# A hybrid attention, HGRN2 and mixture-of-experts layer: weights split by halves, experts gathered from x, slots 64 to 95 gathered in a branch, a ring of 20 pieces

## The chip, the cores and the metric

The kernel runs on one core of a Trainium2 chip. The metric is the device time of one execution in microseconds, and less is better. Three executions of the kernel before took 1235.04, 1236.87 and 1237.81 us; their median, 1236.87 us, is the time before.

## What is computed

One layer of an encoder over 256 tokens of 1024 channels, all in float32. The first half normalises x, modulates it by a vector c, multiplies it by `w_in` (1024 x 5632), sends the parts through differential attention and a chunkwise HGRN2 recurrence, multiplies both results by `w_branch_a` and `w_branch_b` (512 x 1024), merges them by sigmoid gates and multiplies by `w_out` (1024 x 1024). The second half is a mixture of 32 experts, of which each token takes the best 4:

```python
def expert_block(args):
    toks, e = args
    xb = xf[toks]
    gu = xb @ w_gate_up[e] + b_gate_up[e]
    g, u = jnp.split(gu, 2, axis=-1)
    g = jnp.minimum(g, SWIGLU_LIMIT)
    u = jnp.clip(u, -SWIGLU_LIMIT, SWIGLU_LIMIT)
    glu = g * jax.nn.sigmoid(g * SWIGLU_ALPHA)
    return ((u + 1.0) * glu) @ w_down[e] + b_down[e]
...
h = rms_norm(x, norm_pre_ffn[l]) * (1.0 + sc2) + sh2
y = moe(h, router_w[l], router_b[l], w_gate_up[l], b_gate_up[l], w_down[l], b_down[l])
x = x + g2 * rms_norm(y, norm_post_ffn[l])
```

`w_gate_up` of one expert is 1024 x 2048 and `w_down` 1024 x 1024, 12 MiB together, so the experts' weights are 384 MiB.

## The kernel before

**The ring.** All large weights arrive in pieces of 128 x 2048 float32, 1 MiB each. `piece(i)` is one of 16 tiles of the arena (`NA`) or one of `NM` = 2 more in the pool `mo`, which takes the memory of the pool `late` once that is closed (L863). The deque `slots` holds the numbers of the pieces in use as a ring: `chunk` (L84) takes the next one through `spot` and issues a DMA from SyncE's queue at L87. SyncE's queue is in order, so an issue that waits for its piece to be free holds up all issues behind it. In the token mixer the ring is short (`use(8, 9, 6, 10, 3)`, L358), because other pieces hold intermediate results; it grows by `slots.insert` as these die: 3, 5, 2, 4, 0, then 1 and 6 after the branch projections, then 14, 15, 11, 12, 13 and 7 (L861) and the two of `mo` when the mixer is over. For the experts it has 18 pieces.

**The mixer.** A float32 weight is split into a rounded part `hi` and a rest `lo`, and each product is three matmuls of the type float32r (`mm3`, L139 to L141). `split` (L116) does a whole piece at a time: a copy on ScalarE (L119) into one of three tiles `hi`, a subtraction on VectorE (L122) into one of the pieces 11, 12 and 13. `split_between` (L125) does the same in two halves at three places. `proj` (L301) then goes through a piece at a time, and for each through both blocks of 128 tokens. The router's end is L776 to L846: transposes, logits, the largest four, and `posm`, the place (1, 2, ...) of each token among those of its expert. At L833 ScalarE writes `xn2`, the second norm of x, 128 x 2 x 1024.

**The experts.** Expert e's tokens are taken out of `xn2` by a matmul with a one-hot matrix. `onehot` (L898) compares `posm` with a row of numbers on VectorE for two experts at a time and for 96 places of each (`CA` = 96, `EB` = 2); `gather` (L910) then multiplies: 128 x 128 blocks of `xn2` are the weights, 192 one-hot columns move. ScalarE and VectorE (L907, L908) scale the result into `xg`. The gathers for the experts e+2 and e+3 are put as `fill` between the two products of the experts e and e+1, two quarters each (experts 0 and 1 do it otherwise: L1099 and the list `first` for experts 0 and 1, all four quarters for experts 2 and 3 in expert 1).

The number of tokens of an expert is read into registers of TensorE, ScalarE and VectorE by `load(e + 1)` (L1105) behind the fills of expert e. Branches then choose the work. Up to 32 tokens take the path of 32 (L958, L983), more the path of 64 (L948, L975), and those from 65 to 96 take a second path of 32 besides (`po`, `so`, `gdo`). A count over 96 goes to `rare`. Per expert there are two halves of `gate_up`, each followed by its branches (L1158, L1164), the fills, the load of the next count, then under branches (L1191, L1195) the transposes of the activations (L967) and of the gates (`turned`, L997), `down` and the combination (`combine`, L1000: matmuls at L1007 and sums into `acc` on VectorE at L1010). `step` and `in_turn` write TensorE's order out by hand: halves, fills, load, down. The PSUM pools are `psa` (4 banks), `psb` and `psc` (2 each): `turned` and the first transposes take theirs from `psc` and `psb`, as the four banks of `combine` do.

```python
pcs = [bank((psc, psb)[c // 2], NT, 256) for c in range(4)]
order = range(4) if n == U else (0, 2, 1, 3)
...
for g in fill:
    in_turn(g)
if e < NE - 1:
    after = in_turn(lambda: load(e + 1))
    wd = down_loads(e)
```

## Time and profile before

| | |
|---|---|
| median of three runs | 1236.87 us |
| the profiled execution | 1234.81 us |
| its span, first to last instruction | 1232.7 us |
| TensorE busy | 1003.6 us (81%) |
| VectorE / ScalarE busy | 422.8 us (34%) / 225.4 us (18%) |
| moved by DMA | 465.70 MB, 378 GB/s over the span |
| granted TensorE clock, mean | 0.933 of full speed |

The profiled execution is 2.06 us under the median. PE is TensorE's matmuls, PEld its weight loads, DVE is VectorE, ACT ScalarE, SPq the queue of SyncE that issues the DMAs. An "idle before" in square brackets is the time in which an engine did nothing ahead of a row, with what ended it. A matmul in float32 stands in the trace as two instructions. [...]

### The profile page before, as it was taken

What the parts mean: (1) busy time and instruction counts of PE and PEld (TensorE: products, weight loads), DVE (VectorE), ACT (ScalarE), POOL (GpSimd) and SP (SyncE); (2) the same over time, 40 slices, a digit from 0 to 9 for tenths busy, and PEclk for the clock granted to TensorE, in tenths of its full rate; (3) what the DMA queues carried; (4) which work ended last, traced back from release to release, by engine and by line L of the source; (5) the groups of instructions that cost most, each with busy time, mean ns of one, the idle gap of its engine ahead of it and who ended that gap; (6) DMA issues with size and microseconds to landing.
All of it is one profiled execution on the core that took longest, in us unless ns stands there. A gap on an engine that the chain in (4) does not pass through costs nothing. (4 is left out here: it accounts for less than half of the span.)

```text
span 1232.7 us, 17243 instructions
## 1 busy us (share of the span) xinstructions
PE 1003.6 (81%) x6774; PEld 520.9 (42%) x6774; DVE 422.8 (34%) x784; ACT 225.4 (18%) x401; POOL 26.0 (2%) x36
## 2 busy tenths in 40 slices
PE   6999989998779998887789879769776667777855
PEld 3777777874334333333333334323232222233312
DVE  3597789642222222323222232312222212122212
ACT  3553565341111000110000010000010000010001
POOL 1020000010000000000000000000000000000000
PEclk9998989989899999998999999988999887889978
DMA  9966668699999999799999999999999999999994
GB/s 352 317 220 226 230 244 319 263 374 379 394 421 422 423 422 422 308 403 377 422 421 423 422 422 422 423 422 425 422 421 421 423 422 422 416 415 421 419 417 173
DMA packets 100191, 465.70 MB, mean 378 GB/s; under 512 B 9716, under 2 KB 9814, under 8 KB 67256
## 3 DMA queue, kind: packets, MB, share of 16 engines
q1 hardware_dynamic: 100024, 463.31, 93.1%
q8 instruction: 125, 2.05, 0.6%
q14 instruction: 42, 0.34, 0.1%
HBM read 462.23 MB, written 1.05 MB: 376 GB/s over the span
## 5 line engine op out<-in xcount | busy, mean ns | idle before, releaser
L958 PE MATMUL bank<-piece,xg 128*32 128x512 f32 x1472 | 206.6, 673 | 65.0 <-DMA piece<-in_w_gate_up_dram 51.2
L948 PE MATMUL bank<-piece,xg 128*64 128x512 f32 x768 | 171.0, 597 | 3.8 <-PEq L1158 3.0
L1010 DVE TENSOR_TENSOR acc<-acc,bank 128x512 f32<-128x512 f32 x136 | 84.3, 681 | 247.0 <-PE bank L1007 247.0
L926 DVE TENSOR_SCALAR bank<-bank 128x256 f32<-128x256 f32 (+1 forms) x35 | 18.3, 524 | 368.2 <-PE bank L958 254.6
L958 PEld LDWEIGHTS bank<-piece,xg 128*32 128x32 f32 x1472 | 44.4, 116 | 204.7 <-DMA piece<-in_w_gate_up_dram 112.0
L948 PEld LDWEIGHTS bank<-piece,xg 128*64 128x64 f32 x768 | 56.1, 138 | 112.0 <-issue 101.0
L983 PE MATMUL bank<-piece,actT 128*32 128x256 f32 x1472 | 99.5, 421 | 4.1 <-DMA piece<-in_w_down_dram 2.0
L927 ACT ACTIVATE s<-bank 128x256 f32<-128x256 f32 (+1 forms) x32 | 14.8, 463 | 476.5 <-DVE bank L926 476.5
L916 PEld LDWEIGHTS bank<-oh,xn 128*128 128x128 f32 x512 | 86.2, 200 | 30.6 <-issue 20.8
L916 PE MATMUL bank<-oh,xn 128*128 128x192 f32 (+1 forms) x512 | 95.4, 342 | 0.4 <-DVE xg L908 0.4
L975 PE MATMUL bank<-piece,actT 128*64 128x512 f32 x384 | 85.0, 595 | 0.9
L139 PE MATMUL bank<-hi,piece 128*128 128x512 f32 x208 | 82.5, 403 | 2.5 <-ACT hi L119 2.5
L140 PE MATMUL bank<-piece 128*128 128x512 f32 x208 | 82.6, 397 | 2.1 <-DVE piece L122 2.1
L141 PE MATMUL bank<-hi,piece 128*128 128x512 f32 x208 | 82.6, 397 | 0.0
L983 PEld LDWEIGHTS bank<-piece,actT 128*32 128x32 f32 x1472 | 49.8, 121 | 48.4 <-issue 16.7
L967 PE MATMUL bank<-ident,s 128*128 128x128 f32 x88 | 16.9, 298 | 62.8 <-issue 30.5
L122 DVE TENSOR_TENSOR piece<-piece,hi 128x2048 fp32r<-128x2048 f32 x27 | 62.7, 2324 | 14.3 <-ACT hi L119 14.3
L1007 PE MATMUL bank<-y,gt 32*128 32x256 f32 (+1 forms) x544 | 49.2, 396 | 21.3 <-ACT y L1026 21.3
L119 ACT CAST hi<-piece 128x2048 fp32r<-128x2048 f32 x27 | 51.2, 1900 | 18.9 <-PE bank L141 16.2
L1007 PEld LDWEIGHTS bank<-y,gt 32*128 32x128 f32 (+1 forms) x544 | 33.4, 185 | 44.5 <-ACT y L1026 42.4
L975 PEld LDWEIGHTS bank<-piece,actT 128*64 128x64 f32 x384 | 26.5, 137 | 51.7 <-issue 46.8
L1026 ACT COPY y<-bank 128x256 f32<-128x256 f32 (+1 forms) x35 | 15.6, 445 | 176.8 <-PE bank L983 95.0
(267 smaller groups left out, 884.9 us busy)
## 6 DMA issues: line engine op xcount, KB each, us to landing
piece<-in_w_gate_up_dram SPq DMA_DIRECT2D x256, 1024.0 KB, 19.7
piece<-in_w_down_dram SPq DMA_DIRECT2D x128, 1024.0 KB, 19.6
piece<-in_w_in_dram SPq DMA_DIRECT2D x22, 1024.0 KB, 6.3
piece<-in_w_mod_dram SPq DMA_DIRECT2D x16, 1024.0 KB, 6.4
piece<-in_w_mod_dram SPq DMA_DIRECT2D x16, 512.0 KB, 6.9
piece<-in_w_out_dram SPq DMA_DIRECT2D x4, 1024.0 KB
piece<-in_w_branch_b_dram SPq DMA_DIRECT2D x2, 1024.0 KB
piece<-in_w_branch_a_dram SPq DMA_DIRECT2D x2, 1024.0 KB
```

The source lines that it names most:

```text
L119: (seq if order else now)(A, lambda: nc.scalar.copy(hi, v))
L122: (seq if order else now)(V, lambda: nc.vector.tensor_tensor(lo, v, hi.bitcast(F32), ALU.subtract))
L139: nc.tensor.matmul(out, ah, bh, start=start, stop=False, skip_group_check=True)
L140: nc.tensor.matmul(out, ah, bl, start=False, stop=False, skip_group_check=True)
L141: return nc.tensor.matmul(out, al, bh, start=False, stop=stop, skip_group_check=True)
L916: last = nc.tensor.matmul(ph[:, j], xn2[:, t, k * P : (k + 1) * P], oh[:, t, cs], start=t == 0, stop=t == NT - 1)
L948: nc.tensor.matmul(pp[r : r + C], xg[:, k, :C], wg[k][:, 0, 512 * q : 512 * (q + 1)], start=False, stop=k == KD - 1, skip_group_check=True)
L958: nc.tensor.matmul(halves(po[U * q : U * q + U]), xg[:, k, s0 : s0 + U], quarter(wg[k][:, 0], q), start=False, stop=k == KD - 1, skip_grou ...
L975: nc.tensor.matmul(py[C * n : C * n + C], at[:, j, C * half : C * half + C], wd[kk // 2][:, kk % 2, 512 * n : 512 * (n + 1)], start=kk == ...
L983: nc.tensor.matmul(py[U * c : U * c + U, 0:256], at[:, j, U * q : U * q + U], wd[kk // 2][:, kk % 2, 256 * c : 256 * (c + 1)], start=kk == ...
L1007: nc.tensor.matmul(pcs[c][:, t], gt[r : r + n, t * P : (t + 1) * P], y[r : r + n, w : w + 256], start=True, stop=True)
L1010: nc.vector.tensor_tensor(acc[:, :, cs], acc[:, :, cs], pcs[c], ALU.add)
```

## The change

The ring has two pieces more; several tiles are smaller, moved or gone, and the order of some work is another.

- `split` always works by halves: `hi` and `lo` are tiles of 128 x 1024 with four buffers each, both in `late`, so that pieces 11, 12 and 13 are no longer taken. 12 and 13 join the mixer's ring at once, and 11 holds what `xn2` held and joins after the branch projections. `proj`, the branch projections and the first half of `w_out` go through their weights by pairs of 128 rows, and for each pair through both blocks of tokens.
- `xn2` after the router is gone: the gather multiplies x, and the one-hot holds each token's factor `r2` in place of 1.
- `onehot` and `gather` cover 64 places of each of two experts (128 columns, not 192). Places 64 to 95 are gathered by `gather_more` into `xo`, under a branch of its own behind the load of the next expert's count (`ahead`).
- `NM` is 4; `w2` is made in expert 30 in a buffer of `xg`.
- `turned` writes to a bank of `psa`, and the combination of the path of 32 goes in the order 2, 0, 3, 1.

```diff
@@ -40,7 +40,7 @@
-NM = 2
+NM = 4
@@ -109,30 +109,20 @@
-    now = lambda engine, f: f()
-
-    parts = deque((11, 12, 13))
-
-    def split(v, n, m, order=False):
-
-        hi = late.tile([P, 2048], F32R, name="hi", bufs=3).rearrange("p (a b) -> p a b", b=m)
-        (seq if order else now)(A, lambda: nc.scalar.copy(hi, v))
-        lo = piece(parts[0], F32R).rearrange("p (a b) -> p a b", b=m)
-        parts.rotate(-1)
-        (seq if order else now)(V, lambda: nc.vector.tensor_tensor(lo, v, hi.bitcast(F32), ALU.subtract))
-        return hi, lo
-
-    def split_between(v, m, before):
-
-        hi = late.tile([P, 2048], F32R, name="hi", bufs=3).rearrange("p (a b) -> p a b", b=m)
-        lo = piece(parts[0], F32R).rearrange("p (a b) -> p a b", b=m)
-        parts.rotate(-1)
+    def split(v, before=None, order=False):
+
+        now = seq if order or before else lambda engine, f: f()
+        parts = [], []
         for i in range(2):
-            before(i)
+            if before:
+                before(i)
+            hi, lo = (late.tile([P, 2, 512], F32R, name=n, bufs=4) for n in ("hi", "lo"))
             h = slice(2 * i, 2 * i + 2)
-            seq(A, lambda: nc.scalar.copy(hi[:, h], v[:, h]))
-            seq(V, lambda: nc.vector.tensor_tensor(lo[:, h], v[:, h], hi[:, h].bitcast(F32), ALU.subtract))
-        return hi, lo
+            now(A, lambda: nc.scalar.copy(hi, v[:, h]))
+            now(V, lambda: nc.vector.tensor_tensor(lo, v[:, h], hi.bitcast(F32), ALU.subtract))
+            for part, t in zip(parts, (hi, lo)):
+                part.extend((t[:, 0], t[:, 1]))
+        return parts
@@ -182,7 +172,8 @@
-    xn2 = const.tile([P, NT, D], F32, name="xn2")
+    xn2 = part(11, 0, NT, D)
+    r2 = const.tile([P, NT], F32, name="r2")
@@ -293,19 +284,19 @@
-        for kh, (wh, wl) in enumerate(w):
+        for K in range(0, KD, 2):
+            wh, wl = w[K // 4]
...
-                for k in range(4):
-                    K = 4 * kh + k
-                    mm3(pp[t], (hTh[:, K, ts], hTl[:, K, ts]), (wh[:, k], wl[:, k]), K == 0, K == KD - 1)
+                for k in (K, K + 1):
+                    mm3(pp[t], (hTh[:, k, ts], hTl[:, k, ts]), (wh[k % 4], wl[k % 4]), k == 0, k == KD - 1)
@@ -369,8 +360,8 @@
-    wf = split_between(wf, 512, lambda i: normed_split(2 + i, f[i]))
-    wq = split_between(win_chunk(3, 1), 512, lambda i: None)
+    wf = split(wf, lambda i: normed_split(2 + i, f[i]))
+    wq = split(win_chunk(3, 1), order=True)
@@ -698,14 +689,17 @@
-        wb, wa = [split(chunk(rows(a[w], 0, 4)[:, :, ns], 4, 512), 4, 512) for w in ("w_branch_b", "w_branch_a")]
+        wb, wa = [split(chunk(rows(a[w], 0, 4)[:, :, ns], 4, 512)) for w in ("w_branch_b", "w_branch_a")]
+        for (wh, wl), (yh, yl), sig in ((wb, yT[0], sigb), (wa, yT[1], siga)):
+            pp = [bank(psa) for t in range(NT)]
+            for h0 in range(0, H, 2):
+                for t in range(NT):
+                    ts = slice(t * P, (t + 1) * P)
+                    for h in (h0, h0 + 1):
+                        last = mm3(pp[t], (yh[:, h, ts], yl[:, h, ts]), (wh[h], wl[h]), h == 0, h == H - 1)
+            for t in range(NT):
+                nc.vector.tensor_tensor(sig[:, t, ns], pp[t], sig[:, t, ns], ALU.mult)
         for t in range(NT):
-            ts = slice(t * P, (t + 1) * P)
-            for (wh, wl), (yh, yl), sig in ((wb, yT[0], sigb), (wa, yT[1], siga)):
-                pp = bank(psa)
-                for h in range(H):
-                    last = mm3(pp, (yh[:, h, ts], yl[:, h, ts]), (wh[:, h], wl[:, h]), h == 0, h == H - 1)
-                nc.vector.tensor_tensor(sig[:, t, ns], pp, sig[:, t, ns], ALU.mult)
@@ -713,6 +707,7 @@
+    slots.insert(4, 11)
@@ -800,8 +795,10 @@
+    for K in range(0, KD, 2):
+        for t in range(NT):
+            times(t, (K, K + 1))
     for t in range(NT):
-        times(t, range(KD))
@@ -827,10 +824,8 @@
-    r21 = rstd(mx[:, 1])
+    r21 = rstd(mx[:, 1], r2[:, 1:2])
     largest(0, pl0, r20)
-    for t, r2 in enumerate((r20, r21)):
-        seq(A, lambda: nc.scalar.activation(xn2[:, t], x[:, t], AF.Copy, scale=r2))
@@ -858,14 +853,14 @@
-    for i, t in enumerate((14, 15, 11, 12, 13, 7)):
+    for i, t in enumerate((14, 15, 7)):
...
-        slots.insert(8 + i, NA + i)
+        slots.insert(5 + i, NA + i)
@@ -892,20 +887,21 @@
-        return nc.vector.tensor_tensor(oh, iota[:, None, s0 : s0 + n].to_broadcast([P, ne, n]),
-                                       posm[:, t, e0 : e0 + ne].unsqueeze(2).to_broadcast([P, ne, n]), ALU.is_equal)
-
-    def onehot(e0, ne, s0, n):
-        oh = mo.tile([P, NT, EB, CA], F32, name="oh")
-        oh = oh.rearrange("p t e c -> p t (e c)")[:, :, : ne * n].rearrange("p t (e c) -> p t e c", c=n)
+
+        for i in range(ne):
+            last = nc.vector.tensor_scalar(oh[:, i], iota[:, s0 : s0 + n], posm[:, t, e0 + i : e0 + i + 1], r2[:, t : t + 1], ALU.is_equal, ALU.mult)
+        return last
+
+    def onehot(oh, e0, ne, s0, n):
+        oh = oh.rearrange("p t c -> p (t c)")[:, : NT * ne * n].rearrange("p (t e c) -> p t e c", t=NT, c=n)
...
-        nc.scalar.activation(xg[:, k, cs], ph[:, 0], AF.Identity, bias=sh2[:, k : k + 1], scale=sa2[:, k : k + 1])
-        nc.vector.tensor_scalar(xg[:, k + 1, cs], ph[:, 1], sa2[:, k + 1 : k + 2], sh2[:, k + 1 : k + 2], ALU.mult, ALU.add)
+        nc.scalar.activation(xg[:, k, cs], ph[0], AF.Identity, bias=sh2[:, k : k + 1], scale=sa2[:, k : k + 1])
+        nc.vector.tensor_scalar(xg[:, k + 1, cs], ph[1], sa2[:, k + 1 : k + 2], sh2[:, k + 1 : k + 2], ALU.mult, ALU.add)
@@ -913,14 +909,24 @@
-                last = nc.tensor.matmul(ph[:, j], xn2[:, t, k * P : (k + 1) * P], oh[:, t, cs], start=t == 0, stop=t == NT - 1)
-        gathered(ph, xg, kp, cs)
+                last = nc.tensor.matmul(ph[:, j], x[:, t, k * P : (k + 1) * P], oh[:, t, cs], start=t == 0, stop=t == NT - 1)
+        gathered([ph[:, 0], ph[:, 1]], xg, kp, cs)
...
-        xg = mo.tile([P, KD, EB * CA], F32, name="xg")
-        oh = onehot(e0, EB, 0, CA)
+        xg = mo.tile([P, KD, EB * C], F32, name="xg")
+        oh = onehot(mo.tile([P, NT, EB * C], F32, name="oh"), e0, EB, 0, C)
         return xg, [lambda kp=kp: gather(oh, xg, kp) for kp in range(KD // 2)]
+
+    def gather_more(e, xo):
+
+        oh = onehot(mo.tile([P, NT, U], F32, name="oho", bufs=1), e, 1, C, U)
+        ph = [bank(psc, KD // 2, U) for i in range(2)]
+        for k in range(KD):
+            for t in range(NT):
+                nc.tensor.matmul(ph[k % 2][:, k // 2], x[:, t, k * P : (k + 1) * P], oh[:, t], start=t == 0, stop=t == NT - 1)
+        for kp in range(KD // 2):
+            gathered([ph[i][:, kp] for i in range(2)], xo, kp, slice(0, U))
@@ -1000,7 +1006,7 @@
-        order = range(4) if n == U else (0, 2, 1, 3)
+        order = (2, 0, 3, 1) if n == U else (0, 2, 1, 3)
@@ -1020,15 +1026,15 @@
-        turned(gd, gt, bank(psc) if pt is None else pt)
+        turned(gd, gt, pt)
@@ -1129,25 +1134,38 @@
-    after = load(0)
-    fin = pt = other = None
+    def ahead(e):
+
+        cnt = in_turn(lambda: load(e))
+        xo = mo.tile([P, KD, U], F32, name="xo", bufs=1)
+        with tc.If(cnt > C) as more:
+            gather_more(e, xo)
+        step(more.cond_inst)
+        return cnt, xo
+
+    after = ahead(0)
+    fin = other = None
...
-        cnt = after
+        cnt, xo = after
...
-        if e == LASTS:
-            w2 = mo.tile([P, D], F32, name="w2", bufs=1)
-            for n, pr in enumerate(rows_of(gw2, psc)):
-                nc.scalar.copy(w2[:, 512 * n : 512 * (n + 1)], pr)
...
+            if e == NE - 2:
+                w2 = mo.tile([P, KD, EB * C], F32, name="xg").rearrange("p a b -> p (a b)")
+
+                def gated_rows():
+                    for n, pr in enumerate(rows_of(gw2, psc)):
+                        nc.scalar.copy(w2[:, 512 * n : 512 * (n + 1)], pr)
+
+                fill = [gated_rows]
...
-        xe = xg[:, :, j * CA : (j + 1) * CA]
+        xe = xg[:, :, j * C : (j + 1) * C]
@@ -1156,7 +1174,7 @@
-                gate_up_32(e, po, xe, wg, ks, C)
+                gate_up_32(e, po, xo, wg, ks)
@@ -1182,10 +1200,11 @@
-            after = in_turn(lambda: load(e + 1))
+            after = ahead(e + 1)
...
-            pt, other = bank(psa), bank(psa)
+            other = bank(psa)
+        pt = bank(psa)
```

## Rows read from the trace of the kernel before

**Rows 1.** The page's slices of the span, 40 of 30.8 us: DMA in tenths, GB/s
```profile
DMA  9966668699999999799999999999999999999994
GB/s 352 317 220 226 230 244 319 263 374 379 394 421 422 423 422 422 308 403 377 422 421 423 422 422 422 423 422 425 422 421 421 423 422 422 416 415 421 419 417 173
```

**Rows 2.** Windows: span, busy time of PE, PEld, DVE, ACT, POOL, clock, DMA share, GB/s
```profile
30.00:262.00 232.00, 219.85 (x1119) 176.27 (x1118) 171.29 (x233) 114.77 (x152) 17.70 (x12) 0.96 0.74 265
...
160.00:170.00 10.00, 9.12 (x34) 8.01 (x35) 7.95 (x16) 4.64 (x10) 0.00 (x0) 0.50 0.67 205
...
375.00:557.00 182.00, 164.26 (x1038) 69.64 (x1030) 46.67 (x92) 17.67 (x39) 0.00 (x0) 1.00 0.97 400
...
510.00:520.00 10.00, 7.34 (x84) 3.69 (x78) 2.90 (x5) 1.12 (x3) 0.00 (x0) 1.00 0.30 126
530.00:540.00 10.00, 9.68 (x47) 3.19 (x44) 0.00 (x0) 0.00 (x0) 0.00 (x0) 1.00 0.96 361
560.00:570.00 10.00, 8.38 (x56) 2.50 (x60) 0.15 (x1) 0.00 (x0) 0.00 (x0) 0.69 0.75 288
600.00:1200.00 600.00, 451.68 (x3441) 191.11 (x3443) 140.49 (x298) 54.45 (x129) 0.00 (x0) 0.92 1.02 421
```

**Rows 3.** Waits of SyncE's queue, 500 to 580 us: in total, times, longest
```profile
SPq L87 <- PE bank L975: 28.5, 8, 14.2
...
SPq L87 <- PE bank L958: 13.6, 7, 8.7
```

**Rows 4.** Timeline of PE, experts 7, 8 and 9: start, us
```profile
504.46 2.87 PE L916 MATMUL bank<-oh,xn 128*128 128x192 f32 x16
...
508.53 0.41 PE L997 MATMUL bank<-ident,gdo 128*128 128x128 f32 x2 [0.99 <-DVE xg L908]
...
516.27 0.63 PE L967 MATMUL bank<-ident,s 128*128 128x128 f32 x4 [2.05 <-DVE acc L1010]
...
546.38 0.63 PE L967 MATMUL bank<-ident,s 128*128 128x128 f32 x4 [1.26 <-DVEq L1191]
...
561.11 0.62 PE L938 MATMUL bank<-bgu,sel 96*32 96x512 bf16 x4 [3.98 <-issue]
561.51 5.98 PE L958 MATMUL bank<-piece,xg 128*32 128x512 f32 x32
```

**Rows 5.** Timeline of PE, experts 0 and 1: gathers of 96 and of 192 columns
```profile
289.83 2.02 PE L916 MATMUL bank<-oh,xn 128*128 128x96 f32 x16
...
314.69 5.71 PE L916 MATMUL bank<-oh,xn 128*128 128x192 f32 x32
```

**Rows 6.** Groups of the experts, 265 to 1233 us: busy us, mean ns, idle before
```profile
L1010 DVE TENSOR_TENSOR acc<-acc,bank 128x512 f32<-128x512 f32 x136 | 84.3, 681 | 247.0 <-PE bank L1007 247.0
...
L927 ACT ACTIVATE so<-bank 128x256 f32<-128x256 f32 x3 | 1.1, 383 | 57.5 <-DVE bank L926 57.5
```

**Rows 7.** Branches on PE, line 1195: duration ns least/median/most
```profile
L1195 PEldq COMPARE_BRANCH  x44: 65/218/5052, 294.5 to 1212.7; - x44
```

**Rows 8.** Groups of the mixer, 0 to 265 us: busy us, mean ns, idle before
```profile
L122 DVE TENSOR_TENSOR piece<-piece,hi 128x2048 fp32r<-128x2048 f32 x27 | 62.7, 2324 | 14.3 <-ACT hi L119 14.3
L119 ACT CAST hi<-piece 128x2048 fp32r<-128x2048 f32 x27 | 51.2, 1900 | 18.9 <-PE bank L141 16.2 <-DMA piece<-in_w_in_dram 2.6
...
L134 DVE TENSOR_TENSOR piece<-piece,hi 128x1024 fp32r<-128x1024 f32 x6 | 7.2, 1220 | 0.4 <-ACT hi L133 0.3
L133 ACT CAST hi<-piece 128x1024 fp32r<-128x1024 f32 x6 | 6.1, 1042 | 0.0
```

**Rows 9.** Timeline of PE in the mixer: two waits for a split, products in a row
```profile
158.62 0.72 PE L139 MATMUL bank<-hi,piece 128*128 128x512 f32 x2 [2.47 <-ACT hi L119]
...
197.18 0.50 PE L140 MATMUL bank<-piece 128*128 128x512 f32 x1 [1.74 <-DVE piece L122]
197.52 0.39 PE L141 MATMUL bank<-hi,piece 128*128 128x512 f32 x1
197.75 0.39 PE L139 MATMUL bank<-hi,piece 128*128 128x512 f32 x1
```

More of the change, by code (lines that the diff above doesn't have):

```diff
@@ L295, in win_half @@
     def win_half(i, kh, order=False):
-        return split(win_chunk(i, kh), 4, 512, order)
+        return split(win_chunk(i, kh), order=order)
     def win(i, order=False):
@@ L316, in proj_T @@
                 K = 4 * kh + k
-                last = mm3(pp[h // 2][:, h % 2], (wh[:, k, hs], wl[:, k, hs]), (hTh[:, K], hTl[:, K]), K == 0 and h % 2 == 0, K == KD - 1)
+                last = mm3(pp[h // 2][:, h % 2], (wh[k][:, hs], wl[k][:, hs]), (hTh[:, K], hTl[:, K]), K == 0 and h % 2 == 0, K == KD - 1)
         return last
@@ L357 @@
     wf = win_chunk(4, 1)
-    use(8, 9, 6, 10, 3)
+    use(12, 13, 8, 9, 6, 10, 3)
     ph = [transposed_cols(xn2, kp, psc) for kp in (2, 3)]
@@ L730, in w_out_half @@
         ns = slice(512 * n, 512 * (n + 1))
-        wo = [split(chunk(rows(a["w_out"], 512 * kh, 4)[:, :, ns], 4, 512), 4, 512) for kh in range(2)]
+        wo = [split(chunk(rows(a["w_out"], 512 * kh, 4)[:, :, ns], 4, 512)) for kh in range(2)]
         def times(t, ks):
@@ L1027, in out_of, with rest_of @@
         combine(gt, y, n) if fin is None else combine_into(fin, gt, y, n)
-    def rest_of(e, s0, xr, spare):
-        ring = deque(spare[1:])
+    def rest_of(e, s0, spare):
+        ring = deque(spare[2:])
         def half(w, kh, n):
@@ L1038, in half @@
             return v
-        oh = onehot(e, 1, s0, P)
+        xr = part(piece(spare[1]), 0, KD, P)
+        oh = onehot(mo.tile([P, NT, EB * C], F32, name="oh"), e, 1, s0, P)
         for kp in range(KD // 2):
@@ L1083, in rare @@
                 with tc.If(cnt > CA):
-                    rest_of(e, CA, xr, spare)
+                    rest_of(e, CA, spare)
                     with tc.If(cnt > CA + P):
-                        rest_of(e, CA + P, xr, spare)
+                        rest_of(e, CA + P, spare)
         return some
-    xg = mo.tile([P, KD, EB * CA], F32, name="xg")
-    oh = mo.tile([P, NT, EB, CA], F32, name="oh")
+    xg = mo.tile([P, KD, EB * C], F32, name="xg")
+    oh = mo.tile([P, NT, EB * C], F32, name="oh")
     for t in range(NT):
-        seq(V, lambda: slot_is(oh[:, t], t, 0, EB, 0, CA))
+        seq(V, lambda: slot_is(oh[:, t].rearrange("p (e c) -> p e c", c=C), t, 0, EB, 0, C))
     count()
-    oh = oh.rearrange("p t e c -> p t (e c)")
-    ph = [bank((psc, psb)[kp % 2], 2, CA) for kp in range(KD // 2)]
+    ph = [bank((psc, psb)[kp % 2], 2, C) for kp in range(KD // 2)]
     for t in range(NT):
         for k in range(KD):
-            seq(T, lambda: nc.tensor.matmul(ph[k // 2][:, k % 2], xn2[:, t, k * P : (k + 1) * P], oh[:, t, 0:CA], start=t == k % 2 == 0,
+            seq(T, lambda: nc.tensor.matmul(ph[k // 2][:, k % 2], x[:, t, k * P : (k + 1) * P], oh[:, t, 0:C], start=t == k % 2 == 0,
                                             stop=t == NT - 1, skip_group_check=True))
     for kp in range(KD // 2):
-        gathered(ph[kp], xg, kp, slice(0, CA))
-    first = [lambda kp=kp: gather(oh, xg, kp, CA) for kp in range(KD // 2)]
+        gathered([ph[kp][:, 0], ph[kp][:, 1]], xg, kp, slice(0, C))
+    first = [lambda kp=kp: gather(oh, xg, kp, C) for kp in range(KD // 2)]
     softmax()
```

17 lines of the change are left out of this document (8 added, 9 removed).

## The prediction

> **What bounds the kernel now.** I read the page's slices first [rows 1]. From the tenth slice to the last but one DMA runs at nine tenths or more, with one dip (308 GB/s in the 17th) and two smaller ones beside it. So the experts go at the pace of the loads, and a gain has to come from times in which no load is under way. Between 600 and 1200 us the mean is 421 GB/s [rows 2], and no slice there is under 415 [rows 1]; a piece of 1 MiB (1.0486 MB) then takes 2.49 us. Against that rate the window 510 to 520 lacks 10 x (421 - 126) / 421 = 7.0 us, 530 to 540 lacks 1.4 and 560 to 570 lacks 3.2 [rows 2]. Behind 570 the end is set by the bytes left.
>
> What keeps loads from being issued there? SyncE's queue waits for TensorE, up to 14.2 us at a time, at the lines of the products [rows 3]: the ring is full, and load n goes out only when TensorE has let go of piece n - 18. In the stretch before, 375 to 557 us, TensorE is busy for 164.26 of 182 us at the full clock [rows 2]. It is the bound there because two of the three experts with over 64 tokens [rows 6] follow each other (experts 6 and 7; rows 4 show the second path of 7, and 6 has the same rows 44 us earlier), with experts of 33 to 64 around them. The last hold is at expert 9, after TensorE stood idle for 3.98 us ahead of a branch's work and then went through 32 instructions in 5.98 us [rows 4] at a mean clock of 0.69 [rows 2].
>
> In the mixer, 30 to 262 us, TensorE is busy for 219.85 of 232 us and DMA at 265 GB/s [rows 2]. There TensorE is the bound, and what loads do ahead of it is limited by the ring.
>
> So the time is: TensorE's progress at 561 us, less what the ring holds, plus the rest of the bytes. I take the change's parts by what they do to these. Minus is earlier.
>
> **The ring, -5.0.** With 20 pieces the load n waits for piece n - 20. If TensorE is as far as before at the last hold, two loads more are out: 2 x 2.49 = 5.0 us. That holds whatever the mixer does, since all 20 are in use long before 510 us. The three pieces that join the mixer's ring early give no second gain: what they bring sooner is the same lead. Ends: 0, if the hold moves behind other waits, and -5.0.
>
> **The gathers, -7.6.** 16 instructions with 192 columns take 2.87 us [rows 4], 16 with 96 columns 2.02 us [rows 5], so at 96 columns the width no longer counts alone. 128 columns lie between 2.02 and 2.87; by their columns they would take 2.87 x 128 / 192 = 1.91. I take 2.02, since 1.91 is nearest to it. Expert 1's four quarters go from 5.71 [rows 5] to 4.04 us (-1.7); experts 2 to 8 gain 0.85 each (-5.9). Ends: 0 and -8.5. The first gather of all, 32 instructions too, I put at 0, with the one-hot's four smaller VectorE instructions in place of two ahead of it; `xn2`'s ScalarE work at L833 lies beside the router's chain and is worth nothing.
>
> **The gather behind a branch, +11.** Experts 6 and 7 need it, in the turns of experts 5 and 6. It is 16 products, 32 instructions; at 2.02 / 16 a piece 4.0 us [rows 5]. It also waits: the one-hot stands on VectorE behind the last scaling of the fill, whose end now costs TensorE 1.26 us [rows 4] and is paid again, and the transposes behind it need a bank of `psc` that four small scalings must first empty. I take 1.5 us for both and so 5.5 each. Ends: 4.0 and 8.0 each, 8 and 16 together.
>
> **Skipping it, +3.6.** The branch is met ten times up to the last hold (for experts 0 to 9), and eight times it jumps. A branch takes 218 ns at the median [rows 7], and each jump is followed by semaphore instructions; but the longest took 5052 ns [rows 7]. The 3.98 us of rows 4 are such a case. I take 0.45 us a jump, about twice the median. Behind the jump stand L967 and `down`, and with them the release of four pieces. Ends: 1.8 (the median) and 3.6 + 4.0 (one long one more).
>
> **Banks, -4.0.** `turned` in `psa` no longer waits for the last scaling in `psc`: 0.99 us [rows 4] for each of the two experts. With the order 2, 0, 3, 1 the transposes wait for the first or the second of four sums of 681 ns [rows 6], not for the third: of 2.05 us [rows 4] about 1.0 goes. Twice 2.0. Ends: -1 and -5. `turned` takes the bank of `psa` that was spare; each expert now uses all four, but the next expert's first one has been empty since the activations, so this costs 0.
>
> **The mixer, -2.0.** Halves cost 2 x 1220 - 2324 = 116 ns on VectorE and 2 x 1042 - 1900 = 184 ns on ScalarE per piece [rows 8], 27 times: 3.1 and 5.0 us beside TensorE's work, hidden by it (VectorE is busy for 171.29 of 232 us [rows 2]), and dear only where VectorE is already late. What TensorE waits for becomes shorter: the wait of 2.47 us for a copy would lose 1900 - 1042 ns, that of 1.74 us for a subtraction 2324 - 1220 ns [rows 8, 9]: 2.0 us, which I take, though the queues' order changes with it. Buffers: three pieces' worth were ahead before and two now, but in steps of half a size. A piece's 24 products take 5.5 us at 0.23 us from start to start [rows 9]; before, a buffer was free again 16.4 us after its turn began, of which 5.5 are use and 4.2 refill, 6.7 to spare; now 11.0 less 2.7 and 2.3, 6.0 to spare. About even. Ends: +5, if those 0.7 us are missing several times, and -8: the two waits (4.2) and the half-speed stretch around 160 to 170 us (clock 0.50 over 9.12 busy us, some 4 us) [rows 2] that followed the first of them.
>
> `w2` in expert 30, `rare`'s buffers and the new order of the branch projections are off this path or even; all behind 570 us hides under the loads, since TensorE works for 451.68 of 600 us there [rows 2]. If that cover were gone, the 21 other jumps would cost 9.5 us.
>
> **Sum:** -5.0 - 7.6 + 11 + 3.6 - 4.0 - 2.0 = -4.0 us. The profiled execution, 1234.81, would become 1230.8; it lay 2.06 under the median of 1236.87, from which I count: **1232.9 us**, with a range of its own of 1229 to 1236.
>
> **Rivals.**
> - *The stall ahead of expert 9 is gone.* For it: it is one branch of many, most of which take 0.2 us. TensorE is then 3.98 us and the clock's loss (10 x 0.31 = 3.1 us) earlier, but the hold at 510 to 540 us stays and lets through only the 1.4 and 3.2 us behind it: 1232.9 - 4.6 = 1228.3.
> - *The mixer gains all it could*, the -8 above: 1232.9 - 6.0 = 1226.9. For it: the wait and the low clock stand together; against it: other engines' queues are replanned, and a new wait elsewhere does the same. With the first rival too, 1222.
> - *No change.* The gather behind the branch and the jumps take the ring's 5 us: half of the way to their upper ends (+2.5 and +2.0): 1237.4.
> - *Slower: the new branches stall.* The place is the jump between fill and transposes on TensorE. A stall costs 3.98 us [rows 4], and the sum turns when one more than now falls into the stretch up to 561 us; with two or three more (10 us) the time is 1243. Against it: from 375 to 557 us, six experts' branches long, the clock never fell and TensorE lost 18 us in all [rows 2].
>
> [...]
>
> **How the numbers follow.** Forecast 0.46, stall gone 0.13, mixer 0.13, no change 0.11, slower 0.17. A measurement of this kernel tells 0.2% (2.5 us) from none, so 1234.4 and 1239.3 are the bounds. The forecast's own range reaches a little over 1234.4, and some of that goes to no change: faster 0.69, within 0.2% 0.14, slower 0.17. The range of 8 in 10 reaches from both gains together (1222, and 2 below) to the slower case's lower part: 1220 to 1241.
>
> **What would show it.** Right: the wait of SyncE between 500 and 580 us shorter, the windows at 510 and 560 fuller, L916's 16 instructions at 2.0 us with 128 columns, two gathers of 32 instructions into `xo`, and after 600 us 421 GB/s as now. Wrong: long idle times of TensorE ahead of L967 or L938, lower clock after them, a DMA dip after 570 us, or the first expert starting later than at 275 us.

## The result, and the profile after

The changed kernel takes 1268.68 us (1263.87 to 1273.09) against 1236.21 us of the kernel before beside it: ratio 1.0254, interval 1.0228 to 1.0280. It is slower by 32 us, where 4 us less were forecast. The profiled execution took 1263.87 us with a span of 1261.9.

The page's slices of the changed kernel, to be laid beside [rows 1] (40 slices, of 31.5 us here):

```profile
DMA  9977578887999997889999999999999999999994
GB/s 337 333 269 270 185 244 319 333 354 317 388 412 414 414 415 299 331 311 413 413 414 413 413 414 413 414 414 416 414 413 414 412 411 411 405 406 413 409 409 171
```

Two things are new. The one dip of [rows 1] has become three slices at 299, 331 and 311 GB/s (16th to 18th). And where the loads run undisturbed most slices show 411 to 416 GB/s and not 421 to 425.

Windows of the changed kernel (stretch, length, busy time of PE, PEld, DVE, ACT, POOL, clock, DMA share, GB/s), beside [rows 2]:

```profile
30.00:258.00 228.00, 219.49 (x1131) 174.87 (x1130) 173.65 (x263) 120.03 (x180) 18.62 (x13) 0.98 0.77 279
...
510.00:520.00 10.00, 10.00 (x64) 2.85 (x60) 0.00 (x0) 0.00 (x0) 0.00 (x0) 1.00 0.77 280
530.00:540.00 10.00, 7.71 (x97) 4.25 (x99) 3.92 (x9) 1.63 (x5) 0.00 (x0) 1.00 0.45 188
...
600.00:1200.00 600.00, 449.33 (x3442) 191.72 (x3438) 142.24 (x319) 52.73 (x130) 0.00 (x0) 0.89 1.02 412
```

In this execution the mixer is done 4 us sooner and its loads are faster (279 against 265 GB/s). Behind 600 us DMA is as full as before (1.02) but moves 412 GB/s in place of 421.

TensorE of the changed kernel: expert 0, the start of expert 1, the turns of experts 5 and 6, and the start of expert 8 (start, us, what, and the idle time before it):

```profile
271.02 1.06 PE L944 MATMUL bank<-bgu,sel 96*64 96x512 bf16 x4 [0.73 <-PEq L1176]
271.86 8.92 PE L954 MATMUL bank<-piece,xg 128*64 128x512 f32 x32
...
311.66 0.62 PE L944 MATMUL bank<-bgu,sel 96*32 96x512 bf16 x4 [4.07 <-issue]
...
431.13 2.05 PE L912 MATMUL bank<-oh,x 128*128 128x128 f32 x16
434.92 5.95 PE L927 MATMUL bank<-oho,x 128*128 128x32 f32 x32 [1.73 <-DVE oho L892]
442.30 1.09 PE L973 MATMUL bank<-ident,s 128*128 128x128 f32 x4 [1.43 <-DVEq L1210]
...
443.74 8.35 PE L981 MATMUL bank<-piece,actT 128*64 128x512 f32 x32
...
480.07 3.73 PE L927 MATMUL bank<-oho,x 128*128 128x32 f32 x32 [1.48 <-DVE oho L892]
...
484.95 0.45 PE L973 MATMUL bank<-ident,so 128*128 128x128 f32 x1 [1.01 <-DVE xo L904]
...
485.75 6.08 PE L989 MATMUL bank<-piece,actT 128*32 128x256 f32 x64
...
494.38 0.41 PE L973 MATMUL bank<-ident,s 128*128 128x128 f32 x2 [0.85 <-DVE acc L1016]
494.98 0.41 PE L973 MATMUL bank<-ident,s 128*128 128x128 f32 x2 [0.19 <-DVE acc L1016]
...
548.69 0.62 PE L944 MATMUL bank<-bgu,sel 96*64 96x512 bf16 x4 [0.35 <-PEq L1176]
```

Expert 0 begins at 271.0 us, 3.9 sooner than in the profiled execution of the kernel before; expert 8 begins at 548.7 us, 21 later. The rows show four kinds of loss on the way: an idle time of 4.07 us ahead of expert 1, the two gathers behind the branch (5.95 us and 1.73 us of waiting, then 3.73 and 1.48), products that take 8.92 and 8.35 us (granted clock 0.79 and 0.85) where they take 7.09 at the full clock (1.00, the 32 at 281.23), and a longer wait ahead of L973 (1.43 us). They also show what came as forecast: 16 instructions with 128 columns in 2.05 us, and transposes of `s` that wait 0.85 and 0.19 us where they waited 2.05. The 0.99 us of [rows 4] are not gone: 1.01 us stand ahead of the second transpose of `so` now.

SyncE's queue of the changed kernel, 470 to 560 us (in total, times, longest), beside [rows 3]: the ring waits for the products of `down` (L981, L975 before) and of `gate_up` (L954, L948 before). The longest wait is 20.5 us where [rows 3] had 14.2.

```profile
SPq L87 <- PE bank L981: 41.2, 8, 20.5
SPq L87 <- PE bank L954: 39.3, 16, 8.4
```

### The profile page after: what moved, and what is told of

The parts are those of the page before. It is cut to its first block, busy times and chain, and to the rows that moved or that the text cites. A ratio compares the mean times of both kernels' runs of the same rounds, so it can differ in the third digit from the quotient of the medians.

```text
span 1261.9 us, 17756 instructions
## 1 busy us (share of the span) xinstructions
PE 1007.8 (80%) x6870; PEld 524.2 (42%) x6870; DVE 428.0 (34%) x861; ACT 228.4 (18%) x438; POOL 26.7 (2%) x36
## 5 line engine op out<-in xcount | busy, mean ns | idle before, releaser
L964 PE MATMUL bank<-piece,xg 128*32 128x512 f32 x1280 | 171.5, 652 | 49.3 <-DMA piece<-in_w_gate_up_dram 34.6
L954 PE MATMUL bank<-piece,xg 128*64 128x512 f32 x768 | 171.4, 599 | 3.0 <-PEq L1176 2.7
L989 PE MATMUL bank<-piece,actT 128*32 128x256 f32 x1472 | 116.9, 478 | 17.1 <-issue 16.5
L964 PEld LDWEIGHTS bank<-piece,xg 128*32 128x32 f32 x1280 | 38.5, 115 | 165.5 <-issue 89.3
L954 PEld LDWEIGHTS bank<-piece,xg 128*64 128x64 f32 x768 | 56.5, 138 | 111.3 <-issue 101.6
L973 PE MATMUL bank<-ident,s 128*128 128x128 f32 x88 | 19.7, 331 | 86.8 <-issue 46.7
L981 PE MATMUL bank<-piece,actT 128*64 128x512 f32 x384 | 88.3, 612 | 0.5
L989 PEld LDWEIGHTS bank<-piece,actT 128*32 128x32 f32 x1472 | 56.7, 136 | 72.6 <-issue 43.5
L130 PE MATMUL bank<-lo,piece 128*128 128x512 f32 x208 | 84.0, 404 | 3.3 <-DVE lo L122 3.3
L122 DVE TENSOR_TENSOR lo<-piece,hi 128x1024 fp32r<-128x1024 f32 x60 | 74.0, 1253 | 16.4 <-ACT hi L121 16.1
L912 PEld LDWEIGHTS bank<-oh,x 128*128 128x128 f32 x512 | 64.5, 205 | 29.6 <-issue 18.4
L912 PE MATMUL bank<-oh,x 128*128 128x128 f32 (+1 forms) x512 | 70.7, 295 | 1.2 <-DVE xg L904 1.2
L121 ACT CAST hi<-piece 128x1024 fp32r<-128x1024 f32 x60 | 62.0, 1048 | 44.7 <-PE bank L131 36.5
L973 PEld LDWEIGHTS bank<-ident,s 128*128 128x128 f32 x88 | 11.1, 156 | 95.3 <-issue 84.0
```

The source lines that it names most:

```text
L121: now(A, lambda: nc.scalar.copy(hi, v[:, h]))
L122: now(V, lambda: nc.vector.tensor_tensor(lo, v[:, h], hi.bitcast(F32), ALU.subtract))
L130: nc.tensor.matmul(out, ah, bl, start=False, stop=False, skip_group_check=True)
L912: last = nc.tensor.matmul(ph[:, j], x[:, t, k * P : (k + 1) * P], oh[:, t, cs], start=t == 0, stop=t == NT - 1)
L954: nc.tensor.matmul(pp[r : r + C], xg[:, k, :C], wg[k][:, 0, 512 * q : 512 * (q + 1)], start=False, stop=k == KD - 1, skip_group_check=True)
L964: nc.tensor.matmul(halves(po[U * q : U * q + U]), xg[:, k, :U], quarter(wg[k][:, 0], q), start=False, stop=k == KD - 1, skip_group_check=True)
```

## The experiments

Ratios are to the kernel before on the same chip, with 95% intervals. The sum to be explained is that of the kernel and the change run once more side by side.

**base, after_again: both kernels as they are.**

> The kernel before, unchanged, for its profile on the chip of the other runs. Theory A (the lower load rate of the changed kernel, 414 instead of 422 GB/s behind 600 us, comes from the program or its tiles): 421 to 423 GB/s here and about 1236 us. Theory B (it comes from the chip or the moment of the run): here too a rate as low as the changed kernel has beside it.

> The changed kernel, unchanged, on the same chip as the other runs. Theory A: 412 to 414 GB/s behind 600 us, and 1264 to 1273 us again. Theory B: the same rate as the kernel before has here, and a time only 10 to 18 us over it, which is what TensorE's lateness at expert 8 (21 us) less two pieces (5 us) makes.

Measured: 1237.87 us in a single run; 1269.74 us, ratio 1.0272 (1.0245 to 1.0300). Behind 600 us base ran at 421 GB/s and after_again at 412 on the same chip, as theory A had it: the rate belongs to the program. The two stretches to compare everything with, of the kernel before (windows, same columns as above), and the second one of after_again:

```profile
280.00:610.00 330.00, 285.10 (x1928) 126.05 (x1926) 84.96 (x175) 33.99 (x77) 0.00 (x0) 0.97 0.98 398
600.00:1180.00 580.00, 446.17 (x3354) 190.84 (x3350) 138.53 (x291) 54.16 (x127) 0.00 (x0) 0.92 1.02 421
```

```profile
600.00:1180.00 580.00, 432.40 (x3361) 181.14 (x3361) 137.34 (x315) 50.97 (x127) 0.00 (x0) 0.88 1.01 412
```

**narrow: the gathers alone.** The kernel before with the 128-column gathers and the gather behind a branch; ring, mixer, banks and `xn2` as before.

```diff
-    xg = mo.tile([P, KD, EB * CA], F32, name="xg")
+    xg = mo.tile([P, KD, EB * C], F32, name="xg")
...
-    after = load(0)
+    after = ahead(0)
```

> The kernel before with one part of the change alone: 128 columns in the gathers, places 64 to 95 gathered behind a branch; ring, splits, xn2 and banks as before. Theory A (this part is the loss on TensorE: gather with 32 columns, its waits and the low clock behind it, 8 to 9 us for each of experts 6 and 7, and longer jumps): 10 to 20 us slower, 1246 to 1256. Rival (TensorE's lateness comes from the clock and the stalls of experts 0 and 1, which have to do with the mixer's new order): within 5 us of before.

Measured: 1269.6 us, ratio 1.0281 (1.0251 to 1.0312). This part alone loses 34 us, as much as the whole change and more than theory A's 10 to 20. Its loads run at 420 GB/s behind 600 us, so most of its loss lies before that:

```profile
280.00:610.00 330.00, 277.86 (x1850) 125.02 (x1850) 77.27 (x174) 32.55 (x79) 0.00 (x0) 0.91 0.90 363
```

Of 398 GB/s 363 are left and of the mean clock of 0.97 only 0.91. At 421 GB/s the bytes that are missing after 330 us, 330 x 35, take 27 us to make up.

**wide3: all but the gathers.** The changed kernel with gathers of 96 places, without the branch, and 19 pieces.

```diff
-NM = 4
+NM = 3
...
-        xg = mo.tile([P, KD, EB * C], F32, name="xg")
+        xg = mo.tile([P, KD, EB * CA], F32, name="xg")
```

> The changed kernel with the gathers back to 96 places (192 columns) and no branch for them; the memory holds 19 pieces then, not 20. All else as changed. Theory A: TensorE's lateness at expert 8 is mostly gone, and with one piece more than before 2 us come off: 1230 to 1240. Rival: still over 1250, since splits, x in place of xn2 or the banks cause it.

Measured: 1244.28 us, ratio 1.0070 (1.0044 to 1.0096), between the two expectations. TensorE is earlier than in the kernel before at every expert up to 9 (expert 8 begins at 522.3 us, in base at 530.9), and still the kernel is slower: the loads run at 413 GB/s behind 600 us. So there is a second cause, and it is in no term of the prediction.

**mis, mis128, mis256: where the pieces begin.** What does the rest of the change do to the loads? `xn2` (8192 bytes a partition) has left the pool ahead of the ring, and `r2` (8 bytes, stored as 32) has come. By the addresses in the built programs, which the traces do not hold, the first 16 pieces begin at multiples of 512 in the kernel before and 32 bytes past a multiple of 64 in the changed one. The kernel before was therefore run with unused bytes ahead of its ring, and nothing else:

```diff
     mask = const.tile([P, NT, NE], F32, name="mask")
+    const.tile([P, 8], F32, name="pad")
```

(8 words for mis; 32 for mis128, 64 for mis256.)

> The kernel before with nothing changed but 32 unused bytes ahead of the ring, so that its first 16 pieces begin 32 bytes past a multiple of 64 in each partition, as they do in the changed kernel; in the kernel before they begin at multiples of 64. Theory A (where the pieces begin sets the rate of the loads): 413 GB/s in place of 421 behind 600 us, from the first 60 us on, and 600 us of loads at 2% less give 12 to 15 us: about 1250. Theory B (something else that the changed kernel and the 19-piece kernel share takes the rate: the order of the issues, the halves of the splits, more pieces in flight): 421 GB/s and 1236 as before.

> The kernel before with 128 unused bytes ahead of the ring: pieces at odd multiples of 128. If the grid is 256 or 512: 413 GB/s and 1250; if it is 128: 421 GB/s and 1235.

> The kernel before with 256 unused bytes ahead of the ring: pieces at odd multiples of 256. If the grid is 512: 413 GB/s and 1250; if it is 256 or less: 421 GB/s and 1235.

Measured: with 32 bytes 1251.89 us, ratio 1.0140 (1.0117 to 1.0164); with 128 bytes 1251.28, 1.0120 (1.0102 to 1.0138); with 256 bytes 1235.59, 0.9993 (0.9975 to 1.0010). Windows of mis, mis128 and mis256:

```profile
600.00:1180.00 580.00, 443.90 (x3302) 186.69 (x3301) 136.67 (x288) 54.16 (x127) 0.00 (x0) 0.91 1.02 413
```

```profile
600.00:1180.00 580.00, 446.57 (x3308) 186.95 (x3307) 136.67 (x288) 54.27 (x127) 0.00 (x0) 0.91 1.02 414
```

```profile
600.00:1180.00 580.00, 439.02 (x3341) 182.52 (x3339) 136.39 (x289) 53.04 (x125) 0.00 (x0) 0.93 1.02 421
```

DMA is equally full in all three (1.02); it moves 413 and 414 GB/s, 2% less, where the pieces begin 32 and 128 bytes past a multiple of 256, and 421 where they begin at odd multiples of 256. That is worth 15 us here. It is the place written to that was moved; why the rate goes with it, no run shows.

**wide_al, after_al: 64 bytes.** `r2` made 64 bytes long puts the ring at a multiple of 64, which is not one of 256.

```diff
-    r2 = const.tile([P, NT], F32, name="r2")
+    r2 = const.tile([P, 16], F32, name="r2")[:, :NT]
```

> The 19-piece kernel with the wide gather (1244) with its small tile r2 made 64 bytes long in place of 8, which puts the first 16 pieces at multiples of 64 again. Theory A: 421 GB/s behind 600 us and 13 us less: about 1231, below the kernel before by what the mixer, the banks and one piece more give on TensorE (5 us at the start of each expert). Theory B: 413 GB/s and 1244.

> The changed kernel with r2 made 64 bytes long: 20 pieces, the first 16 at multiples of 64. Theory A: 421 GB/s and 12 to 14 us less than 1269: about 1256; what is left, 20 us over the kernel before, is the gather of 64 places and its branch. Rival: the loss to the gather hides the rate, since the loads wait for TensorE up to 600 us anyway: under 8 us less, over 1261.

Measured: 1237.91 us, ratio 1.0020 (1.0008 to 1.0032); and 1266.97, 1.0256 (1.0221 to 1.0291). The rate stayed at 413 GB/s in both, so the grid is not 64. That wide_al is nevertheless 6 us under wide3, where theory B had the same time, stays unexplained; in the traces its TensorE is 4.8 us sooner at expert 7 (474.0 against 478.8 us).

**after_512, wide_512, wide18: all pieces on the grid.** `r2` 512 bytes long, 480 unused bytes behind the loop's tiles and, in after_512, a one-hot of the branch made 512 bytes long put every piece at a multiple of 512, by the same addresses.

```diff
-    r2 = const.tile([P, NT], F32, name="r2")
+    r2 = const.tile([P, 128], F32, name="r2")[:, :NT]
...
+        if e == 0:
+            mo.tile([P, 120], F32, name="pad", bufs=1)
```

> The changed kernel with all 20 pieces at multiples of 512 bytes (r2 made 512 bytes long, the branch's one-hot 512, 480 unused bytes behind the loop's tiles). In the kernel before the first 16 begin at multiples of 512; at multiples of 64 alone the rate stayed at 413 GB/s. Theory A (a coarser grid than 64 bytes sets the rate): 421 to 424 GB/s behind 600 us and 8 to 12 us less than 1267 to 1269: about 1257. Theory B (beside what 32 bytes do to the kernel before, something else of the change takes the rate): 413 GB/s, 1267.

> The 19-piece kernel with the wide gather, all pieces at multiples of 512. Theory A: 421 to 424 GB/s, 10 to 12 us less than the 1238 to 1244 that it took at 413: about 1228, and faster than the kernel before. Theory B: 413 GB/s, 1238 to 1244.

> The kernel of wide_512 with 18 pieces in place of 19: what one piece of the ring is worth when nothing else differs. By the prediction's ring term (1 MB of load, 2.5 us, for each piece): 2.5 us more than wide_512. Rival: the loads are held up by single long waits of up to 20 us at experts 5 to 8, and a piece more shortens each of them: over 5 us more. Second rival: the waits end by TensorE whatever the ring holds: within 1 us.

Measured: the changed kernel 1256.69 us, ratio 1.0180 (1.0153 to 1.0208), at 421 GB/s. The wide gather with 19 pieces 1228.06, 0.9941 (0.9919 to 0.9963), which is faster than both kernels; with 18 pieces 1228.95, 0.9960 (0.9941 to 0.9980), 0.9 us more, with intervals that overlap. Windows of wide_512:

```profile
280.00:610.00 330.00, 281.38 (x1944) 125.02 (x1944) 90.51 (x193) 34.37 (x78) 0.00 (x0) 0.98 0.99 406
```

The loss of 34.2 us (after_again) can now be split by differences of runs: all but the gathers, on the grid, -6.1 us (wide_512); the gathers with their branch +28.6 (1256.69 - 1228.06, which holds the twentieth piece that they make room for); the addresses +11.7 (34.2 of after_again less 22.5 of after_512).

**skip: a branch that is never taken.** What in the gathers costs 29 to 34 us? The kernel before, wide gather and all, with one more branch an expert at the place where the change has it; it holds the gather of 32 places and asks for over 96 tokens, so it always jumps.

```diff
+        with tc.If(cnt > CA) as more:
+            gather_more(e, xo)
...
             after = in_turn(lambda: load(e + 1))
+            over(after, e + 1)
```

> The kernel before with a branch added at the same place, once an expert, that holds the gather of 32 places and that is never taken here (its condition asks for over 96 places); the wide gather stays. It tells the price of jumping over the new code, without its work. Prediction's term: 0.45 us a jump, 8 jumps ahead of the loads' bound, 3.6 us, 1240. Rival (jumps end in stalls, such as the 4.0 us ahead of expert 1 in the narrow kernel): expert 1 begins 4 us later than before, expert 8 8 to 12 us later, time 1244 to 1248. Second rival: the jump lies beside waits that are there anyway: within 2 us of 1236.

Measured: 1260.09 us, ratio 1.0190 (1.0159 to 1.0220): 26 us for code that never runs, more than any of the three expectations had. The branches of skip: its new one (L1148) in the whole run, and one that was there before (L1185) between 300 and 316 us (duration ns least/median/most):

```profile
L1148 PEldq COMPARE_BRANCH  x32: 207/223/907, 272.9 to 1200.7; - x32
...
L1185 PEldq COMPARE_BRANCH  x1: 4141/4141/4141, 309.1 to 309.1; - x1
```

The new jumps themselves are short. But an old branch behind one of them takes 4.1 us, and TensorE stands idle meanwhile, for 4.43 us. Timeline of skip, expert 1:

```profile
306.83 2.00 PE L1021 MATMUL bank<-y,gt 64*128 64x256 f32 x16 [0.74 <-ACTq L1179]
313.25 0.40 PE L952 MATMUL bank<-bgu,sel 96*32 96x512 bf16 x4 [4.43 <-issue]
313.48 5.30 PE L972 MATMUL bank<-piece,xg 128*32 128x512 f32 x32
```

and of the kernel before in base:

```profile
305.62 2.00 PE L1007 MATMUL bank<-y,gt 64*128 64x256 f32 x16 [0.74 <-ACT y L1026]
308.12 0.40 PE L938 MATMUL bank<-bgu,sel 96*32 96x512 bf16 x4 [0.50 <-PEq L1158]
308.34 3.61 PE L958 MATMUL bank<-piece,xg 128*32 128x512 f32 x32
```

The 4 us come with a second loss: behind the idle time the same 32 products take 5.30 us in place of 3.61, at a granted clock of 0.50. Windows of skip: from 280 to 610 us the mean clock is 0.94 where it was 0.97, and the loads lack 19 GB/s, 330 x 19 / 421 = 15 us.

```profile
280.00:610.00 330.00, 278.95 (x1852) 123.63 (x1850) 81.17 (x168) 31.74 (x72) 0.00 (x0) 0.94 0.94 379
...
314.00:317.00 3.00, 3.00 (x20) 0.77 (x16) 0.00 (x0) 0.00 (x0) 0.00 (x0) 0.50 0.32 63
```

That stall is not the whole price. From the start of expert 0 to the start of expert 8, over the same products, base and then skip:

```profile
276.29:530.90 254.61, 220.73 (x1530) 97.47 (x1531) 65.92 (x139) 27.69 (x62) 0.00 (x0) 0.97 0.96 391
```

```profile
277.06:548.32 271.26, 229.70 (x1530) 102.28 (x1531) 65.95 (x139) 27.66 (x61) 0.00 (x0) 0.94 0.91 368
```

TensorE takes 16.7 us longer: it is busy for 9.0 us more, at the lower clock, and idle for 7.7 us more. Base too has long idle times here, three of them (4.77, 1.93 and 3.55 us). Skip has four (4.43, 3.09, 2.49 and 4.70) and longer short waits besides. Two of the four stand in the middle of a run of 64 instructions, with no branch ahead of them (timeline of skip):

```profile
335.31 6.03 PE L997 MATMUL bank<-piece,actT 128*32 128x256 f32 x51 [3.09 <-issue]
...
361.83 3.44 PE L997 MATMUL bank<-piece,actT 128*32 128x256 f32 x27 [2.49 <-issue]
```

Of the 16.7 us 12.2 are there when expert 4 begins (base, then skip):

```profile
379.21 0.62 PE L938 MATMUL bank<-bgu,sel 96*64 96x512 bf16 x4 [0.43 <-PEq L1158]
...
392.15 0.62 PE L952 MATMUL bank<-bgu,sel 96*64 96x512 bf16 x4 [0.43 <-PEq L1179]
```

The profiled executions differ by 22 us. The last group of loads is issued 17 us later (1211.2 against 1194.5 us); the rest lies behind it, where TensorE is idle for 11.16 us ahead of expert 31 and not for 6.50, with a branch of 4.83 us at the end of it.

**skip_short: the same jumps over less code.** The never taken gather is cut to a quarter of its matmuls and copies.

```diff
-        for k in range(KD):
+        for k in range(2):
```

> The kernel before with the never taken branch (1260), its code cut to a quarter: 4 of 16 matmuls, 2 of 8 copies. Theory G (the price goes with the code jumped over): 5 to 8 us over the kernel before, 1240 to 1244. Theory H (it is one more jump, whatever it jumps over): 1254 to 1262. Where the 4 us stall ahead of expert 1 lies then tells whether it is tied to the place of the jump in the code or to its length.

Measured: 1245.28 us, ratio 1.0071 (1.0047 to 1.0095). The price falls from 26 to 9 us with the length of what is jumped over, at the same number of jumps, with the same tiles and banks; theory G had 5 to 8. A shorter branch also moves all code behind it, so length and place are not told apart. The stall ahead of expert 1 is gone (timeline of skip_short):

```profile
308.35 0.40 PE L952 MATMUL bank<-bgu,sel 96*32 96x512 bf16 x4 [0.50 <-PEq L1179]
```

So the price fell with the code, and the wait shows up at a branch behind the new one (4141 ns in skip) and not at it (907 ns at most).

The DMA queues that the profile calls instruction queues tell the same way. The larger of the two in base, skip and skip_short (packets, MB, share of 16 engines):

```profile
q8 instruction: 125, 2.05, 0.6%
...
q8 instruction: 135, 2.21, 0.6%
...
q8 instruction: 128, 2.10, 0.6%
```

With the other one (42, 46 and 44 packets) the branch that is never taken brings 14 packets more (10 of 16 KB and 4 of 8 KB), and a quarter of its matmuls and copies 5. By the queues' name that is code, loaded though it never runs. That these loads are what TensorE waits for at the later branches, and in the middle of its products, is the author's guess from these counts, and not shown.

**merged: the work without the additional branch.** after_512 with the gather moved into the branch that stands ahead of each expert's first products.

```diff
             with tc.If(cnt > C) as more:
+                if ks[0] == 0:
+                    gather_more(e, xo)
                 gate_up_32(e, po, xo, wg, ks)
```

> The changed kernel with pieces at multiples of 512 (1256.7), and the gather of places 64 to 95 moved into the branch that is there already ahead of each expert's first products for over 64 tokens: the same work, one branch less an expert. Theory E (the additional branch an expert is the price, by the stalls that it puts where TensorE has nothing queued and the clock that falls behind them): expert 1 begins 32 to 34 us after expert 0 in place of 40, and 12 to 20 us less: 1237 to 1245. Theory F (the gather's own work at experts 6 and 7 and the fewer columns of the others are the price): within 4 us of 1256.7.

Measured: 1254.41 us, ratio 1.0156 (1.0135 to 1.0176): 2 us less than after_512, as theory F had it, with intervals that overlap. One branch fewer does not help. The same code is jumped over at another branch, which would explain it and is not shown. Expert 1 begins 41 us after expert 0, and the stall ahead of it is there again (timeline of merged):

```profile
310.39 0.62 PE L944 MATMUL bank<-bgu,sel 96*32 96x512 bf16 x4 [4.58 <-issue]
```

The experiment has no clean end: theory E's stall was there without E's branch, and F's reason (the gather's work) is not what skip shows.

**columns: more work than needed.** narrow with 96 columns in the first gather and 128 in the one behind the branch, the surplus unread.

```diff
-        oh = mo.tile([P, NT, 1, U], F32, name="oho", bufs=1)
+        oh = mo.tile([P, NT, 1, P], F32, name="oho", bufs=1)
```

> The kernel with only the narrow gather and its branch (1269.6) with more columns than are needed: the first gather multiplies 96 columns in place of 64 and the gather in the branch 128 in place of 32; what is beyond 64 and 32 is left unread. Theory C (a matmul of 32 or 64 columns lasts as long as one of 96 to 128, and the granted clock falls to half behind the short ones): the first gather lasts 7.1 us as now, the first products of expert 0 fall from 9.3 to 7.1 us, the gather in the branch lasts 4.1 to 5.5 us, and the down products of experts 5 and 6 that follow it fall from 8.9 to 7.1 and from 5.3 to 3.7 us: 7 to 10 us less, about 1261. Theory D (waits, the skipped branches and loading of instructions cost the time, the columns do not matter): within 3 us of 1269.6, and with four times the columns the gather in the branch takes 1 us or more longer.

Measured: 1258.39 us, ratio 1.0179 (1.0155 to 1.0202), 11 us less than narrow by multiplying more; theory C had 7 to 10. Timelines, expert 6's gather and what follows it, narrow:

```profile
440.40 5.53 PE L933 MATMUL bank<-oho,xn 128*128 128x32 f32 x32 [1.37 <-DVE oho L895]
447.13 1.09 PE L981 MATMUL bank<-ident,s 128*128 128x128 f32 x4 [1.21 <-DVEq L1214]
...
448.57 8.90 PE L989 MATMUL bank<-piece,actT 128*64 128x512 f32 x32
```

columns:

```profile
441.69 3.81 PE L933 MATMUL bank<-oho,xn 128*128 128x128 f32 x32 [1.47 <-DVE oho L895]
446.70 0.63 PE L981 MATMUL bank<-ident,s 128*128 128x128 f32 x4 [1.21 <-DVEq L1214]
447.17 0.38 PE L1011 MATMUL bank<-ident,gd 128*128 128x128 f32 x2
447.63 7.09 PE L989 MATMUL bank<-piece,actT 128*64 128x512 f32 x32
```

The window 443 to 452 us of narrow, and then of columns, has the granted clock (third figure from the end, a share of the full one): 0.50 behind the short matmuls, 1.00 behind the long ones.

```profile
443.00:452.00 9.00, 7.79 (x28) 4.94 (x30) 1.39 (x5) 1.93 (x6) 0.00 (x0) 0.50 1.01 418
```

```profile
443.00:452.00 9.00, 7.71 (x51) 4.46 (x51) 1.39 (x5) 1.93 (x6) 0.00 (x0) 1.00 1.01 416
```

With 128 columns the gather, the transposes and the products behind it take 1.7, 0.5 and 1.8 us less at one expert. At expert 0, with 96 columns ahead of them, the first products fall from 9.27 to 7.04 us. So theory C holds. What then is left over the kernel before, 22 us, is no more than what skip lost, 26, and the two intervals overlap. Whether gathers with long columns would gain anything without the jumps, no run shows: from expert 0 to expert 8 TensorE takes 21.9 us longer than in base in columns, 16.7 in skip and 29.4 in narrow. As an estimate, narrow's 29.4 are 16.7 for the jumps, 7.5 for the short columns and 5.2 for the rest, which holds the two gathers' own work.

## Why the prediction was wrong

**Skipping it, +3.6: this step failed.** The prediction priced a jump by the duration of the branch itself (0.45 us) and put its upper end at one long stall more, 7.6. skip measured 26 us. The branch's own 0.22 us was read rightly, but the cost lies elsewhere. The stalls fall on later branches and into runs of products, with TensorE idle (4.43 and 3.09 us in skip): up to expert 8 one long idle time more and longer short waits, 7.7 us, about the term's upper end. The lower clock behind them makes the products 9.0 us longer, and that the term did not count at all. Behind 570 us the prediction took everything to hide under the loads; but expert 31 lies behind the last of them, and it waits some 5 us more. And the price grows with the code jumped over (26 against 9 us), where the step counted jumps. [rows 4] and [rows 7] showed such a stall and the low clock behind it; the term took the stall for its upper end without the clock, and only a rival (the stall ahead of expert 9 gone) counted the clock.

**The slower rival** was right in kind: stalls and the clock. It had 0.17 and 1243 us, against 1256.69 with the pieces on the grid. Its place, the new jump itself, was wrong. The clock that never fell from 375 to 557 us was held against it, but skip loses 12.2 of its 16.7 us ahead of expert 4, which base begins at 379 us: the stretch looked at lies behind most of the loss.

**"Behind 600 us 421 GB/s as now": wrong,** and no term stood for it. The addresses took 11.7 us of the loss, and without them the time would still have been above the range's 1241.

**The gather behind a branch, 5.5 each.** The wait was taken as 1.5 and is 1.5 and 1.7 in the changed kernel. The products were taken as 4.0 and take 5.95 (granted clock 0.60) and 3.73 (1.00); in narrow they take 5.53 and 6.04. Behind them the next products are slower by 1.3 and 2.4 us, also behind the 3.73 (L989 takes 6.08 at a clock of 0.59 where it takes 3.66 at 1.00). With the transposes that makes 8 to 10 us in place of 5.5 at each of the two experts, over the upper end of 8.0 at one of them. With 128 columns the products take 3.81 and nothing behind them is slower.

**The gathers, -7.6.** 128 columns take 2.05 us, as taken (2.02), so 0.8 us an expert came. The first gather, put at 0, brought 2 us of slower products behind it with its 64 columns (8.92 us; 7.04 in columns, with 96). Expert 0's products of `down`, behind gathers of 64 columns, are slower too, 8.81 us where they take 7.09 in base behind 96.

**Banks, -4.0.** In wide_512 the 2.0 us an expert came as forecast: L1003 waits no more, and L973 waits 1.04 us in place of 2.05. In the changed kernel only the second half is left, since the 0.99 us stand ahead of the second transpose of `so` (1.01 and 0.95 us). No term had what stands behind that wait: expert 6's products of `down` take 8.78 us in base and 7.09 in wide_512 and in the changed kernel.

**The mixer, -2.0.** In the four kernels with the new mixer and the wide gather (wide3, wide_al, wide_512, wide18) expert 0 begins at 268.2 to 269.7 us, against 274.9 and 276.3 in the kernel before: the sign was right there and the gain nearer to the end of -8. With the narrow gather it is not steady: 271.0 us in one profiled execution of the changed kernel, 277.1 in the other (after_again), 274.7 in after_512 and 269.2 in merged. Why is open.

**The ring, -5.0 for two pieces.** wide18 and wide_512 differ by 0.9 us in the medians and 0.2% in the ratios, and their intervals overlap: 2.5 us a piece is neither shown nor excluded. One piece, banks and mixer together were forecast at -8.5 us and gave -6.1 in wide_512.

## What to carry to other kernels

Price a branch over rarely needed work by the code that is jumped over (26 us here, 9 with a quarter of its matmuls and copies) and by how long TensorE is idle at the branches behind it (4.43 us ahead of expert 1 in skip), and add what the clock loses after an idle time, which was the larger half here (9.0 of the 16.7 us from expert 0 to expert 8 in skip); a never taken copy of the branch measures it without its work. When a small tile enters or leaves a pool ahead of the load buffers, look at where these begin: here multiples of 256 bytes gave 421 GB/s and places 32, 64 and 128 bytes past them 412 to 414. Take a load rate as unchanged only if the destinations are: 32 unused bytes alone took it from 421 to 413 GB/s (mis).
